# Two steps of a Strassen-like gate-and-up product change places: P3 of the first column group goes ahead of P2 of the second, and the first group's results are turned behind P3 of the second

## The chip, the cores and the metric

One core of a Trainium2 chip runs the whole kernel as one program. The metric is the device time of one execution in microseconds (us); the median of three runs of the kernel before is 1392.69 us (1392.04 to 1393.3).

## The reference, cut to what matters

The model is a two-layer encoder trunk on a sequence of 512 frames of width 1024, all in float32. Layer 0 has a mixer of gated linear attention and RWKV-7, layer 1 has multi-head latent attention; after each mixer stand a layer norm, a dense SwiGLU feed-forward block and another layer norm. The change touches only the first half of the two feed-forward blocks:

```python
gu = x @ w_gate_up                       # (512, 1024) @ (1024, 5632)
gate, up = gu[..., :2816], gu[..., 2816:]
y = (jax.nn.silu(gate) * up) @ w_down    # (512, 2816) @ (2816, 1024)
x = layer_norm(DN_ALPHA * x + y, ln_g, ln_b)
```

## The kernel before, in words

Every float32 product is made of three matmuls on rounded parts: an operand is cast to a high part on ScalarE (`wh`, L191) and the rest is subtracted on VectorE (`wl`, L192), both in `split`; TensorE then takes high times high, high times low and low times high.

`ffn` (L1139) computes gate and up for six groups of columns (`GROUPS`: four of 512, two of 384). For each group it uses a scheme of the Strassen kind with seven products, P1 to P7, in place of eight. `A` (L1161) holds the seven left operands made from quarters of x; those of P3, P5 and P6 lie in `Sh`/`Sl`, the others in `xh`/`xl`. `sink` (L1184) makes them from the transposed rows of x as the layer norm before yields them, on ScalarE and VectorE.

The right operands are weights in three raw tiles for each group: X, Y and Z. `step(name)` (L1273) does one product. Each product has two halves (`k2` = 0 and 1 in `product`, L1224): a half splits 1024 columns of the raw tile and feeds 12 matmuls, the first eight with the high part, the last four with the low part. Once P1, P3, P7 and P6 have split their operand, `more` (L1261) sends a GpSimd DMA for each half that adds further weights from memory into the same raw tile. Y is so used four times in a row: P3 splits it, a DMA adds to it, P7 splits it, a DMA adds, P6 splits it, a DMA adds, P4 splits it. P2 is added to P1's PSUM banks and P4 to P7's.

The split parts have two places each (`wh`, `wl`, `bufs=2`). With `spare` true, every third half (by `count`) goes to a third place called `third`, cut out of two tiles of `hid` (`parts`, L1211).

What a product yields is combined in the second half of `step`: P1 and P3 are copied out on ScalarE, P2 gets its Silu there, and P5, P6 and P4 are combined on VectorE (`dve`, L1270): P6 alone needs eight operations, which end in `w` (finished) and `v`; P4 finishes `v`. `turn(0)` (L1308) then transposes `w` of two row blocks on TensorE into PSUM tiles of tag "s", of which there are two, and ScalarE copies them into `hid` (L1315); `turn(1)` does so with `v`.

`load` fetches X, Z and Y of groups 0 and 1 on SP's queue long before they are used; `begin` does P1 of group 0 inside the stage before; `work` (L1330) does the rest. For groups 2 to 5 the order is P1, P4 of the group before, turn(0), P3, turn(1), P2, loads, P7, P5, P6. Groups 0 and 1 differ, since their P1 and P2 come first of all: then P3, P7, P5, P6 of group 0, and P4 of group 0, turn(0), P3 of group 1, turn(1), loads, P7 of group 1, and so on.

The source gives the order of importance. The framework lists the instructions of each engine by it and by its own estimate of when each is ready, so neighbouring steps can be woven into each other. On the chip each engine then runs its list in that fixed order.

Of the kernel before, what the change touches and what calls it, by code (L numbers as in the profile page):

```python
# [1138 lines left out]
def ffn(g, i, hid, ep):  # L1139
# [179 lines left out]
    gs = [group(j) for j in range(len(GROUPS))]  # L1319
# [10 lines left out]
    def work():  # L1330

        gs[1].step("P1", False)
        gs[0].step("P2", False)
        gs[1].step("P2", False)
        last = len(gs) - 1
        for j, x in enumerate(gs):
            more = j < 4
            if j:
                if j > 1:
                    x.step("P1", more)  # L1340
                gs[j - 1].step("P4", more)
                gs[j - 1].turn(0)
            x.step("P3", more)
            if j:
                gs[j - 1].turn(1)
            if j > 1:
                x.step("P2", more)
            if 0 < j < last:
                gs[j + 1].load("Z")
                gs[j + 1].load("X")  # L1350
                gs[j + 1].load("Y")
            x.step("P7", more)
            x.step("P5", more)
            x.step("P6", more)
        gs[last].step("P4", False)
        return [lambda h=h: gs[last].turn(h) for h in range(2)]

    return Ctx.of(sink=sink, again=again, load=load, begin=begin, work=work)


# [454 lines left out]
```

## Time and profile before

| what | value |
|---|---|
| median of three runs | 1392.69 us |
| profiled execution: its own time | 1392.04 us |
| profiled execution: span | 1390.0 us |
| mean granted TensorE clock | 0.99 |
| PE busy | 1339.4 us (96%) |
| DVE busy | 920.7 us (66%) |
| ACT busy | 686.5 us (49%) |
| POOL busy | 233.4 us (17%) |
| gate-and-up of layer 0 | from about 403 us of the span |
| gate-and-up of layer 1 | from about 1025 to 1260 us |

PE, DVE, ACT and POOL are TensorE, VectorE, ScalarE and GpSimd. A busy share of 96% means little by itself, since matmuls overlap; 512 columns start every 0.23 us at full clock. What counts is where PE waits, for whom, and at which granted clock it runs.

### The profile page before, as it was taken

What the parts mean: (1) busy time and instruction counts of PE and PEld (TensorE: products, weight loads), DVE (VectorE), ACT (ScalarE), POOL (GpSimd) and SP (SyncE); (2) the same over time, 40 slices, a digit from 0 to 9 for tenths busy, and PEclk for the clock granted to TensorE, in tenths of its full rate; (3) what the DMA queues carried; (4) which work ended last, traced back from release to release, by engine and by line L of the source; (5) the groups of instructions that cost most, each with busy time, mean ns of one, the idle gap of its engine ahead of it and who ended that gap; (6) DMA issues with size and microseconds to landing.
All of it is one profiled execution on the core that took longest, in us unless ns stands there. A gap on an engine that the chain in (4) does not pass through costs nothing.

```text
span 1390.0 us, 21743 instructions
## 1 busy us (share of the span) xinstructions
PE 1339.4 (96%) x8382; PEld 1060.7 (76%) x8382; DVE 920.7 (66%) x1704; ACT 686.5 (49%) x1212; POOL 233.4 (17%) x278
## 2 busy tenths in 40 slices
PE   8899999999999999999999999999999899999997
PEld 6577777766677788997888877666677788997886
DVE  3687677644496766667556367988785766667456
ACT  6653344455536455555344346555445455555341
POOL 2230021132311111127301220000001111120000
PEclk9999999989999999999999999999999999999999
DMA  7563343531478787763225321111367787773232
GB/s 243 114 125 60 74 100 72 105 65 46 145 221 198 157 189 166 151 125 97 91 93 157 109 94 47 53 55 46 117 163 190 155 193 167 145 127 93 91 107 90
DMA packets 74328, 168.15 MB, mean 121 GB/s; under 512 B 21232, under 2 KB 22384, under 8 KB 74096
## 3 DMA queue, kind: packets, MB, share of 16 engines
q0 software_dynamic: 21888, 60.83, 26.2%
q1 hardware_dynamic: 51808, 103.83, 22.6%
q10 hardware_dynamic: 528, 2.10, 0.4%
q8 instruction: 66, 1.08, 0.3%
q14 instruction: 38, 0.31, 0.1%
HBM read 163.77 MB, written 2.95 MB: 120 GB/s over the span
## 4 chain that ended last, share of the span: by engine, by line
PE 55%; DVE 4%; DMA 4%; issue 4%; ACT 2%; POOL 1%; SPq 0%; DVEq 0%; ACTq 0%; POOLq 0%
PE ps_g L1236 23%; PE ps_g L186 8%; PE ps_g L185 8%; PE ps_g L187 8%; PE ps_s L1617 3%; DMA raw<-in_w_gu 2%; PE ps_o L1646 2%; PE ps_t L1633 1%; PE ps_s L1314 1%; DMA wl<-in_w_mi 1%; DVE wl L192 1%; ACT wh L191 1%; DVE w L1270 0%; DMA w<-in_w_mo 0%; DVE x L1008 0%
## 5 line engine op out<-in xcount | busy, mean ns | idle before, releaser
L192 DVE TENSOR_TENSOR wl<-raw,wh 128x1024 fp32r<-128x1024 f32 (+1 forms) x116 | 127.6, 1111 | 87.7 <-ACT wh L191 87.7
L191 ACT CAST wh<-raw 128x1024 fp32r<-128x1024 f32 (+1 forms) x116 | 111.6, 967 | 140.7 <-PE ps_g L1236 94.9
L1263 POOL DMA_DIRECT2D raw<-in_w_gu x96 | 83.3, 869 | 496.9 <-DVE wl L192 274.0
L1236 PE MATMUL ps_g<-wh,xh 128*128 128x512 f32 (+1 forms) x312 | 115.9, 372 | 2.1 <-ACT wh L191 2.1
L187 PE MATMUL ps_g<-xh,wl 128*128 128x512 f32 (+2 forms) x296 | 113.2, 382 | 3.3 <-DMA wl<-in_w_even 2.2
L1236 PE MATMUL ps_g<-wh,xl 128*128 128x512 f32 (+1 forms) x312 | 114.8, 368 | 0.0
L185 PE MATMUL ps_g<-xh,wh 128*128 128x512 f32 (+2 forms) x296 | 114.6, 387 | 0.0
L186 PE MATMUL ps_g<-xl,wh 128*128 128x512 f32 (+2 forms) x296 | 113.3, 383 | 0.0
L186 PE MATMUL ps_g<-wl,ah 128*128 128x512 f32 x288 | 112.0, 390 | 0.6 <-DVE wl L192 0.6
L185 PE MATMUL ps_g<-wh,ah 128*128 128x512 f32 x288 | 111.7, 392 | 0.5 <-ACT ah L191 0.4
L187 PE MATMUL ps_g<-wh,al 128*128 128x512 f32 x288 | 110.8, 389 | 0.0
L192 DVE TENSOR_TENSOR wl<-w,wh 128x1024 fp32r<-128x1024 f32 (+2 forms) x79 | 89.4, 1132 | 31.9 <-ACT wh L191 31.4
L191 ACT CAST wh<-w 128x1024 fp32r<-128x1024 f32 (+2 forms) x79 | 76.3, 966 | 61.4 <-PE ps_g L186 36.5
L191 ACT CAST ah<-hid 128x512 fp32r<-128x512 f32 x72 | 43.7, 621 | 98.8 <-PE ps_g L186 98.8
L192 DVE TENSOR_TENSOR al<-hid,ah 128x512 fp32r<-128x512 f32 x72 | 49.4, 697 | 60.7 <-ACT ah L191 60.7
L1236 PE MATMUL ps_g<-wh,Sh 128*128 128x512 f32 (+1 forms) x232 | 87.1, 376 | 0.0
L1236 PE MATMUL ps_g<-wh,Sl 128*128 128x512 f32 (+1 forms) x232 | 86.7, 374 | 0.0
L1236 PE MATMUL ps_g<-wl,xh 128*128 128x512 f32 (+1 forms) x312 | 78.2, 372 | 4.1 <-DVE wl L192 4.1
L215 POOL DMA_DIRECT2D wl<-in_w_even x48 | 41.6, 867 | 227.0 <-ACT wl L214 191.9
L216 ACT CAST wh<-w 128x512 fp32r<-128x512 f32 x64 | 39.4, 618 | 81.2 <-PE ps_g L186 49.4
L187 PEld LDWEIGHTS ps_g<-xh,wl 128*128 128x128 f32 (+1 forms) x296 | 55.8, 189 | 14.9 <-DMA wl<-in_w_even 3.4
L1236 PEld LDWEIGHTS ps_g<-wh,xh 128*128 128x128 f32 x312 | 58.6, 188 | 10.6 <-ACT wh L191 3.2
(462 smaller groups left out, 3293.2 us busy)
## 6 DMA issues: line engine op xcount, KB each, us to landing
raw<-in_w_gu POOLq DMA_DIRECT2D x64, 512.0 KB, 5.6
w<-in_w_dn SPq DMA_DIRECT2D x44, 512.0 KB
raw<-in_w_gu SPq DMA_DIRECT2D x32, 512.0 KB
w<-in_w_even SPq DMA_DIRECT2D x48, 256.0 KB
wl<-in_w_even POOLq DMA_DIRECT2D x48, 256.0 KB, 4.7
raw<-in_w_gu POOLq DMA_DIRECT2D x32, 384.0 KB, 4.8
w<-in_w_gu SPq DMA_DIRECT2D x12, 512.0 KB
raw<-in_w_gu SPq DMA_DIRECT2D x16, 384.0 KB
```

The lines of the kernel that those rows point to most:

```text
L185: nc.tensor.matmul(out, lhsT=wh, rhs=xh, start=first, stop=False)
L186: nc.tensor.matmul(out, lhsT=wh, rhs=xl, start=False, stop=False)
L187: nc.tensor.matmul(out, lhsT=wl, rhs=xh, start=False, stop=last)
L191: c = nc.scalar.copy(h, src)
L192: (eng or nc.vector).tensor_tensor(l, in0=src, in1=h, op=ALU.subtract)
L215: nc.gpsimd.dma_start(l, src, accum_op=ALU.add)
L216: nc.scalar.copy(h, w)
L1236: nc.tensor.matmul(acc[u][:, :n], lhsT=A_[a][:, k, P * u:P * u + P], rhs=w[:, q], start=first and k + a + b == 0, stop=k + b == 4, skip_gr ...
L1263: nc.gpsimd.dma_start(T[k][k2], w[r, q, k2], accum_op=ALU.add)
L1314: nc.tensor.transpose(out=p[:, m * P:(m + 1) * P], in_=y[:, m * P:(m + 1) * P], identity=g.C("ident"))
L1617: nc.tensor.matmul(p[:, :nk], lhsT=Q[:, h % 4, qb * P:(qb + 1) * P], rhs=K[:, h % 4, :nk], start=True, stop=True)
L1646: nc.tensor.matmul(o[64 * e:64 * e + 64, kb * P:], lhsT=Vv[:, kb, (h - 1 + e) * 64:(h + e) * 64], rhs=t[e][kb][:, kb * P:], start=kb == 0, ...
```

## The change

`work` gets P3 of group 0 between the P2 of group 0 and that of group 1; it is no longer the first step of the loop, and its `spare` is now false, so that `third` is first used by a later half. In the round of group 1, `turn(0)` of group 0 no longer stands between P4 of group 0 and P3 of group 1, but behind that P3, directly ahead of `turn(1)`. Groups 2 to 5 keep their order. Both feed-forward blocks use this code.

```diff
         gs[1].step("P1", False)
         gs[0].step("P2", False)
+        gs[0].step("P3", False)
         gs[1].step("P2", False)
         last = len(gs) - 1
         for j, x in enumerate(gs):
             more = j < 4
             if j:
                 if j > 1:
                     x.step("P1", more)
                 gs[j - 1].step("P4", more)
-                gs[j - 1].turn(0)
-            x.step("P3", more)
-            if j:
-                gs[j - 1].turn(1)
+                if j > 1:
+                    gs[j - 1].turn(0)
+                x.step("P3", more)
+                for h in range(0 if j == 1 else 1, 2):
+                    gs[j - 1].turn(h)
             if j > 1:
                 x.step("P2", more)
```

## Rows read from the trace of the kernel before

**Rows 1.** Timeline of PE: start us, us, engine line op, out<-in xcount [idle before <-releaser].

```profile
456.44 1.07 PE L1236 MATMUL ps_g<-third,xh 128*128 128x512 f32 x4
...
458.83 0.63 PE L1314 MATMUL ps_s<-cst,w 128*128 128x128 f32 x4 [1.33 <-DVE w L1270]
460.64 0.63 PE L1314 MATMUL ps_s<-cst,w 128*128 128x128 f32 x4 [1.18 <-DVE w L1270]
461.02 0.51 PE L1236 MATMUL ps_g<-wh,Sh 128*128 128x512 f32 x1
...
468.15 1.03 PE L1314 MATMUL ps_s<-cst,v 128*128 128x128 f32 x8
468.94 0.48 PE L1236 MATMUL ps_g<-third,xh 128*128 128x512 f32 x1
...
1093.39 0.47 PE L1236 MATMUL ps_g<-third,xh 128*128 128x512 f32 x1
```

**Rows 2.** Windows: us, busy (x) of PE, PEld, DVE, ACT, POOL, PEclk, DMA, GB/s.

```profile
457.35:461.02 3.67, 1.17 (x9) 0.83 (x9) 3.67 (x7) 0.59 (x1) 0.00 (x0) 1.00 0.69 239
461.33:464.74 3.41, 3.41 (x10) 2.63 (x8) 3.41 (x6) 1.79 (x3) 1.35 (x2) 0.50 0.44 44
1085.97:1089.38 3.41, 3.41 (x10) 2.64 (x8) 3.41 (x6) 1.55 (x3) 1.59 (x2) 0.50 0.46 54
400.73:403.50 2.77, 2.19 (x17) 1.63 (x15) 2.70 (x5) 2.07 (x4) 0.00 (x0) 1.00 0.79 293
469.00:600.00 131.00, 131.00 (x641) 113.59 (x640) 88.07 (x107) 71.45 (x97) 25.16 (x29) 1.00 0.78 164
```

**Rows 3.** Chain that ended last, 400:545: start us, us, what.

```profile
430.02 1.24 DVE wl L192
...
431.54 5.34 DMA raw<-in_w_gu
...
448.10 5.17 DMA raw<-in_w_gu
```

**Rows 4.** Timeline of DVE.

```profile
426.57 1.22 DVE L192 TENSOR_TENSOR third<-raw,third 128x1024 fp32r<-128x1024 f32 x1
...
460.41 1.22 DVE L192 TENSOR_TENSOR wl<-raw,wh 128x1024 fp32r<-128x1024 f32 x1
...
1047.71 2.36 DVE L192 TENSOR_TENSOR wl<-hid,wh 128x1024 fp32r<-128x1024 f32 x2
...
1051.24 1.22 DVE L192 TENSOR_TENSOR wl<-raw,wh 128x1024 fp32r<-128x1024 f32 x1
...
1068.92 1.22 DVE L192 TENSOR_TENSOR wl<-raw,wh 128x1024 fp32r<-128x1024 f32 x1 [1.51 <-ACT wh L191]
...
1084.81 1.22 DVE L192 TENSOR_TENSOR wl<-raw,wh 128x1024 fp32r<-128x1024 f32 x1
```

**Rows 5.** Timeline of ACT.

```profile
467.40 1.05 ACT L191 CAST third<-raw 128x1024 fp32r<-128x1024 f32 x1 [3.91 <-DMA raw<-in_w_gu]
468.36 1.07 ACT L1291 COPY w<-ps_g 128x512 f32<-128x512 f32 x2
469.31 1.09 ACT L1315 COPY hid<-ps_s 128x512 f32<-128x512 f32 x2
...
1059.57 1.05 ACT L191 CAST third<-raw 128x1024 fp32r<-128x1024 f32 x1 [1.55 <-DMA raw<-in_w_gu]
...
1091.81 1.05 ACT L191 CAST third<-raw 128x1024 fp32r<-128x1024 f32 x1 [3.91 <-DMA raw<-in_w_gu]
```

**Rows 6.** Timeline of POOL.

```profile
1052.75 0.86 POOL L1263 DMA_DIRECT2D raw<-in_w_gu  x1 [0.27 <-DVE wl L192]
...
1072.40 0.86 POOL L1263 DMA_DIRECT2D raw<-in_w_gu  x1 [3.83 <-issue]
```

**Rows 7.** Timeline of PE, two earlier waits.

```profile
402.07 1.15 PE L1181 MATMUL ps_s<-cst,x 128*128 128x128 f32 x8 [0.29 <-ACT full L1172]
...
424.91 0.50 PE L1236 MATMUL ps_g<-third,Sh 128*128 128x512 f32 x1 [0.59 <-ACT third L191]
```

## The prediction, made before the changed kernel ran

> **What bounds the kernel now.** I read the waits of TensorE first, one stage after the other. In gate-and-up nearly all of them lie where groups 0 and 1 meet; from P7 of group 1 on, PE does not idle at all over 131 us of layer 0 [rows 2], and layer 1 looks the same. So whatever moves the start of that P7 moves the end of the kernel by as much, as long as nothing new waits behind it. It starts at 468.94 in layer 0 and at 1093.39 in layer 1 [rows 1].
>
> Ahead of it the timeline of PE shows the wait that the change goes for: turn(0) of group 0 stands still for 1.33 us, does four transposes, waits 1.18 us more for `w`, and only then P3 of group 1 may begin [rows 1]. Between P4's last matmul and P3's first lie 3.67 us with eight transposes in them, and right behind, the granted clock reads 0.50, the 1.2 GHz level, for 3.41 us, in both layers [rows 2]. A half-clock stretch of that length costs half of it, 1.7 us. That is 2.51 us idle and 1.7 us slow for each layer, 8.4 us in all, and a first look would book them.
>
> The chain of waits says otherwise, and it is the view to trust here. In layer 0 it does not run over PE from 430 to 460 us but over raw tile Y of group 0: P3's second half is subtracted at 430.02, its DMA lands 5.34 us after issue at 431.54, P7 casts and subtracts, a DMA again, P6, a DMA issued at 448.10 that takes 5.17, then P4 [rows 3]. Behind P4's last subtraction stand P6's eight VectorE operations, and behind these, at 460.41, the first subtraction of P3 of group 1 [rows 4]. Its DMA in turn frees the cast of P7 at 467.40, for which ScalarE waited 3.91 us [rows 5]. P7 of group 1 can't start before that cast ends at 468.45; it started at 468.94. So with the chain where it is, taking the wait ahead of P3 away would bring less than half a microsecond: PE would wait ahead of P7 instead.
>
> **The change, part by part.** *P3 of group 0 earlier.* The matmuls, casts and DMAs stay the same in number; they move. In layer 0 VectorE is the bound up to about 429 us, and does its subtractions there in a run of four; P3's first half has the third place in it, at 426.57, and the second half comes last, at 430.02 [rows 3, 4]. Now P3 takes the second and third place. Its second half then begins at about 426.57, 3.45 us earlier. Its low part goes to an ordinary place and not to `third`, which needs the low matmuls of P2's second half done; they are four. The two DMAs then follow each other within 1.1 us, and where they do so in layer 1, the second lands later: issued at 1052.75 [rows 6], cast at 1059.57 [rows 5], 6.82 us against 5.34, so 1.48 us are lost. Left: 1.97 us. The bounds are 0 (P3's second half gets no earlier place) and 3.45.
>
> In layer 1 the subtractions of P2 of group 1 at 1047.71 (two of them) stand ahead of those of P3, the last of which is at 1051.24 [rows 4]; exchanged, P3's last stands at 1048.85, 2.39 us earlier. Further down the chain, P6's second half is subtracted by 1070.14 (1068.92 and 1.22) [rows 4], and 0.29 us is what such a DMA needs after its subtraction (1051.24 and 1.22 against 1052.75). It was issued at 1072.40 behind a wait that the profile puts down to nothing [rows 6]: 1.97 us lost. I take it as an accident that does not come back, with 0 as the other bound. Together 4.36 us.
>
> The P2 of group 1 that now stands behind P3 is off the chain. Its Silu on ScalarE frees banks that P6 needs, two products later. PE itself has to wait about as long as before in that stretch, 0.59 us at 424.91 [rows 7]: P3's left operand is among the last things `sink` makes. I count nothing, with 1 us to either side in each layer.
>
> *turn(0) behind P3 of group 1.* PE goes from P4 straight into P3. Its eight high matmuls run at once, its low ones wait for the subtraction behind the eight operations, at 460.41 less 1.97 in layer 0. So part of the old wait comes back inside P3, but off the chain. Then turn(0) finds `w` finished long before.
>
> What is late next is the cast of P7: 467.40 less 1.97 is 465.43, its end 466.48, against a start at 468.94: 2.46 us gained. In layer 1 the cast at 1091.81 [rows 5] goes to 1087.45, its end to 1088.50, against 1093.39: 4.89 us. But turn(1) had been done by then and now hasn't. It needs the two PSUM tiles of turn(0), which ScalarE copies out only behind P7's cast and behind P3's copies of `w`, as rows 5 list them (467.40, 468.36, 469.31). So I place turn(1) among the first matmuls of P7, for its own 1.03 us [rows 1] and 0.29 us of waiting for a tile, as in the one place where four such transposes come in a row [rows 7]. Net: 1.14 us in layer 0, 3.57 us in layer 1, 4.71 us together. If the copies come out ahead of that cast, turn(1) fits into the wait and each layer gains 1.32 more.
>
> *The clock.* From P3's last matmul to P7's first there are now two turns and a wait. P3's end: the subtraction's end (459.66 in layer 0, 1081.67 in layer 1) and 16 matmuls at 0.23 us, so 463.3 and 1085.3; P7 comes 3.2 us later in both. Without matmuls but with transposes, 3.67 us brought the clock down, and 2.77 us (400.73 to 403.50) did not [rows 2]. 3.2 lies between, so I charge one of the two layers with 1.7 us, bounds 0 and 3.4.
>
> The Trainium skill, in "TensorE: Matmul & The Clock Gate", section "Why this matters for your kernels", warns that idle between bursts of matmuls brings the clock back down, which speaks against putting all four turns into one place. The rows agree that a gap does it; by that rule alone both layers pay, and the sum would be 1.3 us of gain.
>
> The skill's "DMA: Bandwidth & Descriptors", section on the anatomy of a DMA through GpSimd, gives 2.0 us plus bytes over 436 per ns, an estimate of 3.2 us for such a half of 512 KB. The trace disagrees, with 5.17 to 5.34 us for these, which add as they write; by the page the chain would not bind, and the sum would be the first rival's.
>
> *The sum.* 4.71 less 1.7 is 3.0 us. The profiled execution took 1392.04 us, so 1389.0; the median lies 0.65 us above it: 1389.7 us.
>
> **Rivals.** *All of it is gained.* The chain moves far enough that PE alone counts: 8.4 us less two waits of 0.29 us for a PSUM tile is 7.8, so 1384.9 us. For it: P3's second half could gain up to 3.45 us in layer 0. Against it: rows 3 leave no slack at any link.
>
> *Nothing comes of it.* The framework had already woven P3's first half into P2 of group 1 (its first matmul at 424.91 [rows 7]), so the first edit is partly there already. If the unexplained 1.97 us come back and both layers pay the clock, 4.71 less 1.97 less 3.4 is 0.7 us slower: 1393.4 us, within 0.2%.
>
> *Slower.* PE's list has turn(1) ahead of P7, while ScalarE's list has the copies of turn(0) behind P7's cast. Then P7 waits for the cast (1.05 us), the two copies of `w` (1.07), those of turn(0) (1.09) and four transposes (0.52): 3.73 us after the DMA lands, 469.2 in layer 0 (0.2 later than before) and 1091.2 in layer 1 (2.2 earlier). Both layers fall to half clock, 3.4 us: 1.4 us slower. With the 1.97 us in layer 1 back, 3.4 us: 1396.1 us. It decides as soon as the chain gains less than about 2.5 us for a layer. For it: rows 5 show that order on ScalarE. Against it: a list made by readiness puts P7's matmuls, free by then, ahead of a transpose that isn't.
>
> **How the numbers follow.** About 0.2% (2.8 us) is what a measurement of this kernel can tell from no change. Forecast 0.43, all gained 0.20, nothing 0.25, slower 0.12. The forecast's own cases run from 1.3 us of gain (both layers slow) to 7.4 (no slow stretch, both turns hidden); 0.29 of its 0.43 gain over 2.8 us. With the first rival that is 0.49 for faster; slower gets 0.11, of the last rival; the rest, 0.40, is within. The range reaches from 1384.3, just past the first rival, to 1393.8, just past the second; the last rival is left out.
>
> **What would show it.** Right: no wait of turn(0) for `w`; P7 of group 1 about 2.5 us (layer 0) and 4.9 us (layer 1) earlier, each right behind its cast; ScalarE still waiting there for a DMA; turn(1) inside P7; P3 split ahead of P2 of group 1. Wrong: P7 of group 1 with its raw tile landed well ahead, or a turn that waits for a ScalarE copy for a microsecond; the slow clock gone in both layers, or there in both; a new gap between P2 of group 1 and P7 of group 0.

## The result, and the profile after

The changed kernel is slower by 0.7%: 1400.73 us median of eight runs (1396.97 to 1406.88) against 1392.68 us of the kernel before in the same rounds, a ratio of 1.007 with a 95% interval of 1.0044 to 1.0097. The forecast was 1389.7 us, in a range up to 1393.8.

The profiled execution took 1405.09 us, with a span of 1403.0, 13.0 us more than before. Not all of that is the change. The clock in the first mixer, which is the same code, granted 0.50 for 20.5 us in this execution and for 10.2 us in that of before; this alone makes some 5 us (10.2 at half speed), and gate-and-up of layer 0 begins 4.6 us later. So I compare by stage: from the first matmul of line 1236 to the first transpose of turn(0) of group 1, by which time all work of group 0 is done. Before, that is 403.50 to 496.26 us in layer 0, 92.76 us. After, it is 97.04 us in layer 0, and in layer 1 it is 99.32 against 95.81 (1024.91 to 1120.72): 4.28 and 3.51 us longer, 7.8 us in all. Outside these two stages the executions differ by 0.6 us more, besides that later start. The windows of the two stages after (columns as in [rows 2]):

```profile
408.13:520.00 111.87, 102.82 (x466) 82.64 (x467) 77.35 (x95) 61.53 (x85) 19.03 (x22) 1.00 0.79 182
1034.11:1150.00 115.89, 105.23 (x477) 84.11 (x476) 79.95 (x102) 62.43 (x87) 17.30 (x20) 1.00 0.70 157
```

The granted clock stays at its upper level throughout: both half-clock stretches of [rows 2] are gone, and with them 3.4 us of slower work, so the waits of PE have grown by more than its time. That does not mean that the change would have gained 3.4 us: before, P7 of group 1 began only 0.49 and 0.53 us behind the end of its cast [rows 1, 5], so a quicker P3 would for the most part have waited there. The waits of PE in layer 0, 425:500, after (us in total, times, longest):

```profile
PE ps_g L1236 <- DVE wl L192: 3.3, 2, 2.2
PE ps_g L1236 <- ACT wh L191: 2.5, 2, 1.4
PE ps_g L1236 <- ACT third L191: 1.9, 1, 1.9
PE ps_s L1314 <- ACT hid L1315: 0.5, 1, 0.5
```

In the same window before there were 2.5 us for `w` and 0.6 for `third`; 3.1 us have become 8.2. The wait of turn(0) for `w` is gone, as the change wants; waits for the split of weights have come in its place. Where they stand on PE, after:

```profile
442.07 0.50 PE L1236 MATMUL ps_g<-wh,xh 128*128 128x512 f32 x1 [1.45 <-ACT wh L191]
...
459.77 0.50 PE L1236 MATMUL ps_g<-wh,xh 128*128 128x512 f32 x1 [1.05 <-ACT wh L191]
...
469.48 1.20 PE L1236 MATMUL ps_g<-wl,Sh 128*128 128x512 f32 x4 [2.15 <-DVE wl L192]
...
473.24 1.03 PE L1314 MATMUL ps_s<-cst,w 128*128 128x128 f32 x8
...
476.16 0.50 PE L1236 MATMUL ps_g<-third,xh 128*128 128x512 f32 x1 [1.88 <-ACT third L191]
...
477.62 1.15 PE L1314 MATMUL ps_s<-cst,v 128*128 128x128 f32 x8 [0.49 <-ACT hid L1315]
```

In order these are P7 of group 0, P4 of group 0, the low part of P3 of group 1, turn(0), P7 of group 1, and turn(1) inside that P7. The last four answer to [rows 1]; they came in the order that was forecast, but later in the stage. The first two were not forecast, and they are new. (The other wait for `wl` in the list, 1.15 us at 430.12, stands where 0.59 us stood before [rows 7], within what the prediction allowed there.) ScalarE's timeline after tells why the first two came:

```profile
440.02 1.05 ACT L191 CAST third<-raw 128x1024 fp32r<-128x1024 f32 x1 [3.48 <-DMA raw<-in_w_gu]
440.97 1.99 ACT L191 CAST wh<-raw 128x1024 fp32r<-128x1024 f32 x2
...
458.68 1.04 ACT L191 CAST wh<-raw 128x1024 fp32r<-128x1024 f32 x1 [5.15 <-DMA raw<-in_w_gu]
461.17 1.05 ACT L191 CAST third<-raw 128x1024 fp32r<-128x1024 f32 x1 [1.45 <-DMA raw<-in_w_gu]
...
475.06 1.04 ACT L191 CAST third<-raw 128x1024 fp32r<-128x1024 f32 x1 [3.77 <-DMA raw<-in_w_gu]
```

The cast at 440.02 is that of P7's second half, the first user of `third` now; the cast of P7's first half comes behind it, at 440.97. Layer 1 shows the same swap (1066.68 and 1067.63). The DMA of the second half is issued last and lands last, and the first half's cast waits for it, though its own DMA, issued at 431.74, landed 5.8 us later, 3.4 us ahead of that cast. Before, ScalarE cast the first half (the first of the two at 433.58) ahead of the second:

```profile
433.58 2.01 ACT L191 CAST wh<-raw 128x1024 fp32r<-128x1024 f32 x2 [1.81 <-DMA raw<-in_w_gu]
...
436.90 1.05 ACT L191 CAST third<-raw 128x1024 fp32r<-128x1024 f32 x1 [0.35 <-DMA raw<-in_w_gu]
```

The order on POOL after:

```profile
431.74 0.85 POOL L1263 DMA_DIRECT2D raw<-in_w_gu  x1 [14.09 <-ACT wh L191]
432.93 0.86 POOL L1263 DMA_DIRECT2D raw<-in_w_gu  x1 [0.34 <-DVE wl L192]
442.62 0.86 POOL L1263 DMA_DIRECT2D raw<-in_w_gu  x1 [8.83 <-DVE third L192]
443.75 0.86 POOL L1263 DMA_DIRECT2D raw<-in_w_gu  x1 [0.28 <-DVE wl L192]
453.17 0.86 POOL L1263 DMA_DIRECT2D raw<-in_w_gu  x1 [8.55 <-DVE third L192]
455.08 0.86 POOL L1263 DMA_DIRECT2D raw<-in_w_gu  x1 [1.05 <-DVE wl L192]
469.72 0.86 POOL L1263 DMA_DIRECT2D raw<-in_w_gu  x1 [13.78 <-DVE wl L192]
```

P3's two DMAs go out early, at 24.80 us of the stage for the second, against 28.04 before. But P7's are issued 1.13 us apart and in the wrong order, the second half first. Before, they stood 3.31 us apart, the first half first:

```profile
436.19 0.86 POOL L1263 DMA_DIRECT2D raw<-in_w_gu  x1 [3.79 <-DVE wl L192]
439.50 0.86 POOL L1263 DMA_DIRECT2D raw<-in_w_gu  x1 [2.46 <-DVE third L192]
```

P6's first half now waits for the later of the two: its cast stands at 450.56, 6.81 us behind the DMA issued at 443.75.

### The profile page after: what moved, and what is told of

Same layout as the page of the kernel before. It is cut to its first block, busy times and chain, and to the rows that moved or that the text cites. A ratio compares the mean times of both kernels' runs of the same rounds, so it can differ in the third digit from the quotient of the medians.

```text
span 1403.0 us, 21752 instructions
## 1 busy us (share of the span) xinstructions
PE 1343.7 (96%) x8382; PEld 1061.9 (76%) x8382; DVE 921.0 (66%) x1704; ACT 684.8 (49%) x1212; POOL 229.7 (16%) x278
```

## The experiments

The table gives the time of the stage, measured as above in one profile each, the half-clock stretches that lie in it (3.41 us each, 1.7 us of slower work), and the ratio of device times to the kernel before, timed beside it. No kernel was profiled twice, so how far a stage varies by itself is not known; half-clock stretches come and go between the rows, and differences of a microsecond or less should not be read. The intervals of the times are some 3 to 6 us to each side.

| kernel | layer 0, us | layer 1, us | sum less before | half-clock stretches | ratio (95%) |
|---|---|---|---|---|---|
| before | 92.76 | 95.81 | 0 | 1 and 1 | |
| changed | 97.04 | 99.32 | +7.8 | 0 and 0 | 1.007 (1.0044 to 1.0097) |
| e1 | 96.13 | 97.67 | +5.2 | 1 and 2 | 1.0032 (1.0007 to 1.0057) |
| e2 | 93.08 | 96.12 | +0.6 | 1 and 1 | 1.0023 (0.9995 to 1.0051) |
| e3 | 93.02 | 94.70 | -0.9 | 1 and 0 | 0.9994 (0.9966 to 1.0022) |
| e4 | 94.86 | 97.11 | +3.4 | 1 and 1 | 1.0017 (0.9988 to 1.0046) |
| e5 | 88.63 | 91.10 | -8.8 | 0 and 1 | 0.9938 (0.9915 to 0.9962) |
| e6 | 87.70 | 89.48 | -11.4 | 0 and 0 | 0.9936 (0.9896 to 0.9976) |
| e7 | 93.12 | 94.55 | -0.9 | 0 and 1 | 0.9988 (0.996 to 1.0015) |
| e8 | 94.71 | 95.96 | +2.1 | 0 and 1 | 1.0034 (1.0007 to 1.0062) |

**e1, the first edit alone** (against the kernel before):

```diff
         gs[0].step("P2", False)
+        gs[0].step("P3", False)
         gs[1].step("P2", False)
...
-            x.step("P3", more)
             if j:
+                x.step("P3", more)
                 gs[j - 1].turn(1)
```

> Only the first edit: P3 of group 0 ahead of P2 of group 1; turn(0) stays ahead of P3 of group 1. Theory A (order of the casts: with `third` idle, ScalarE's list has the cast of P7's second half, whose DMA lands last, ahead of that of its first half): P7 of group 0 starts about 2.4 us late, P4 waits 1 to 2 us for its cast, and the kernel is 5 to 8 us slower than before. Theory B (the move of turn(0) is what costs): no slower than before, 0 to 3 us faster.

5.2 us slower by stage, 1.0032 in time (some 4 us). In layer 0 ScalarE has the same swapped casts, and P7 of group 0 waits for its cast as after the change, with turn(0) where it was before (waits of PE, 420:490):

```profile
440.89 1.05 ACT L191 CAST third<-raw 128x1024 fp32r<-128x1024 f32 x1 [3.79 <-DMA raw<-in_w_gu]
441.84 1.99 ACT L191 CAST wh<-raw 128x1024 fp32r<-128x1024 f32 x2
```

```profile
PE ps_g L1236 <- ACT wh L191: 2.4, 2, 1.8
PE ps_s L1314 <- DVE w L1270: 2.4, 2, 1.2
PE ps_g L1236 <- DVE wl L192: 1.1, 1, 1.1
```

So theory A holds for the first edit, which makes 5.2 of the 7.8 us by itself.

**e2, the second edit alone** (against the kernel before):

```diff
                 gs[j - 1].step("P4", more)
-                gs[j - 1].turn(0)
+                if j > 1:
+                    gs[j - 1].turn(0)
             x.step("P3", more)
             if j:
-                gs[j - 1].turn(1)
+                for h in range(0 if j == 1 else 1, 2):
+                    gs[j - 1].turn(h)
```

> Only the second edit: turn(0) of group 0 behind P3 of group 1, P3 of group 0 where it was. Theory A: within 2 us of before; P7 of group 1 waits for its cast, whose DMA lands at the same time as before, and P7 of group 0 starts as before. Theory B: 6 to 8 us slower, as the full change.

0.3 us slower in each layer by stage, and in time no change is within the interval; both half-clock stretches are back. The waits in layer 0, 420:490:

```profile
PE ps_g L1236 <- DVE wl L192: 2.1, 1, 2.1
PE ps_g L1236 <- ACT third L191: 0.8, 2, 0.6
PE ps_s L1314 <- ACT hid L1315: 0.5, 1, 0.5
```

The 2.51 us of turn(0) have become 2.1 us inside P3 of group 1 and 0.5 us of turn(1). The second edit moves a wait and removes none. Theory B falls. By stage e1 and e2 make 5.9 us together; the other 2.0 come only when both edits meet, and were not taken apart.

**e3, the full change with `third` for P2 of group 1:**

```diff
         gs[0].step("P3", False)
-        gs[1].step("P2", False)
+        gs[1].step("P2")
```

> The full change, but P2 of group 1 may use `third` for its first half, so that P7's second half has to wait for that place and its cast is listed behind that of the first half. Theory A: P7 of group 0 loses its 1.2 to 1.5 us wait for the cast, the DMAs of its halves go out apart again, and the kernel is 2 us slower to 4 us faster than before, so 6 to 12 us faster than the full change. Theory B: no more than 2 us faster than the full change.

The whole loss is gone: 8.6 us less than the full change by stage. The ninth half, the first of P2 of group 1, now takes `third`; the twelfth, P7's second, has to wait until TensorE is done with it. ScalarE casts in the right order, and the DMAs of P7 (432.60 and 435.15) stand apart again:

```profile
430.00 1.05 ACT L191 CAST wh<-raw 128x1024 fp32r<-128x1024 f32 x1 [2.45 <-DMA raw<-in_w_gu]
430.95 1.07 ACT L1291 COPY w<-ps_g 128x512 f32<-128x512 f32 x2
432.55 1.05 ACT L191 CAST third<-raw 128x1024 fp32r<-128x1024 f32 x1 [0.53 <-PE ps_g L1236]
```

```profile
432.60 0.86 POOL L1263 DMA_DIRECT2D raw<-in_w_gu  x1 [4.96 <-DMA raw<-in_w_gu]
435.15 0.86 POOL L1263 DMA_DIRECT2D raw<-in_w_gu  x1 [1.70 <-DVE third L192]
```

P7's first half is cast 28.89 us into the stage, against 32.84 after the change and 30.08 before.

**e4, the full change with P7 of group 0 in ordinary places:**

```diff
-            x.step("P7", more)
+            x.step("P7", more and j > 0)
```

> The full change, but P7 of group 0 uses the ordinary places for both halves, so that its casts are listed in order with `third` still idle until then. Theory A: the 1.2 to 1.5 us wait ahead of P7 of group 0 gets shorter by at least 1 us, and the kernel is 3 to 10 us faster than the full change. Theory B: within 2 us of the full change.

4.4 us less than the full change by stage, though with two half-clock stretches that the changed kernel doesn't have. `third` idles until a later product, the order of the casts is put right, and P7's wait is gone. The cast of its first half comes 29.68 us into the stage:

```profile
430.15 1.05 ACT L191 CAST wh<-raw 128x1024 fp32r<-128x1024 f32 x1 [1.25 <-DMA raw<-in_w_gu]
432.64 1.05 ACT L191 CAST wh<-raw 128x1024 fp32r<-128x1024 f32 x1 [1.43 <-DMA raw<-in_w_gu]
```

So the swapped order costs, and it isn't all: e4 stays 3.4 us above before, where e3 does not.

**e8, the kernel before with P3 of group 0 in ordinary places:**

```diff
-            x.step("P3", more)
+            x.step("P3", more and j > 0)
```

> The kernel before, with P3 of group 0 in the ordinary places; nothing moved. Theory A: `third` is idle until P7 here too, but P3 stands between, so the casts of P7 are listed in order: within 1.5 us of before. Rival (the lost third place is what costs): 3 to 8 us slower than before.

Not within 1.5 us: 2.1 us by stage, 1.0034 in time. In layer 0 both halves of P3 now wait for an ordinary place and are cast together. The first half's DMA goes out 28.06 us into the stage, against 24.58 before, and the second's 1.14 us behind it instead of 3.46, so that P7 waits 1.7 us for its cast (waits of PE, 420:490):

```profile
PE ps_s L1314 <- DVE w L1270: 2.4, 2, 1.2
PE ps_g L1236 <- ACT wh L191: 1.7, 1, 1.7
PE ps_g L1236 <- ACT third L191: 0.7, 1, 0.7
```

So the lost third place costs by itself, as the rival has it, though by stage less than the rival's 3 to 8 us, and less than e1 with its swapped casts (5.2). The times, 1.0034 and 1.0032, do not tell the two apart. In layer 1 it costs next to nothing (0.15 us).

**e7, the first edit alone with `third` for P2 of group 1:** e1 with the edit of e3.

> Only the first edit, as e1, with `third` for P2 of group 1. Theory A: turn(0) of group 1 comes 2 to 4 us earlier in each layer than in e1, and no later than before; the kernel is 0 to 4 us faster than before. Rival (P3 early itself is late, by the missing third place for P3 or by `sink`): within 2 us of e1, so 3 to 6 us slower than before.

0.9 us faster by stage, 0.9988 in time, whose interval includes no change; 6.1 us better than e1 by stage. In layer 0 turn(0) of group 1 comes 0.36 us later than before, where theory A had it no later. Beside e3 (-0.9) it shows what the second edit brings once the casts are in order: nothing that can be seen. The waits for `w` of 1.04 and 1.18 us in e7 are 0.68 us for P3's low part, 1.69 us for P7's cast and 0.5 us for a tile of turn(1) in e3.

**e6, P3 of group 1 ahead of P4 of group 0**, P3 of group 0 where it was before:

```diff
-            acc[name] = p = acc[chained] if chained else banks(name == "P5" or name == "P1" and j != 1)
+            acc[name] = p = acc[chained] if chained else banks(name == "P5" or name == "P1" and j != 1 or name == "P3" and j == 1)
...
-            if j:
-                if j > 1:
-                    x.step("P1", more)
+            if j == 1:
+                x.step("P3", more)
+                gs[0].step("P4", more)
+                gs[0].turn(0)
+            elif j:
+                x.step("P1", more)
                 gs[j - 1].step("P4", more)
                 gs[j - 1].turn(0)
-            x.step("P3", more)
-            if j:
+            if j != 1:
+                x.step("P3", more)
+            if j > 1:
                 gs[j - 1].turn(1)
...
             x.step("P7", more)
+            if j == 1:
+                gs[0].turn(1)
```

> P3 of group 0 where it was before, P3 of group 1 ahead of P4 of group 0 as in e5. If the chain binds: 4 to 9 us faster than before, within 2 us of e5. If P3 of group 0 has to go early for that: at least 3 us slower than e5.

The first line puts P3 of group 1 into the two PSUM banks of P5. By the count, `third` also goes to P3's second half where P4's had it.

1376.13 us against 1387.54 of the kernel before beside it, 0.9936 in time (some 9 us); 11.4 us less by stage, which is more than the 4 to 9 us expected. All waits at the meeting of the groups are gone; of PE's waits in layer 0, 420:490, one line is left, the old one ahead of P3 of group 0 [rows 7]:

```profile
PE ps_g L1236 <- ACT third L191: 0.6, 1, 0.6
```

P3 of group 1 needs nothing from tile Y of group 0, so it is split, and its matmuls begin (446.19), while the second of P6's DMAs for P4 (issued at 442.24) is still under way. Its own DMAs go out well before P7 of group 1 needs them, and P6's eight VectorE operations have P3 and P4 to hide behind. ScalarE's cast for P7 of group 1, in e6, stands ahead of turn(0)'s copies and is done 4.4 us before PE needs it (P7 begins at 457.86):

```profile
452.36 1.06 ACT L191 CAST third<-raw 128x1024 fp32r<-128x1024 f32 x1 [3.11 <-DMA raw<-in_w_gu]
...
457.71 0.59 ACT L1315 COPY hid<-ps_s 128x512 f32<-128x512 f32 x1 [0.29 <-PE ps_s L1314]
```

Layer 1 gains more (6.33 us against 5.06): there PE had also waited 1.45 us for the cast of P4 of group 0 before, and in e6 it does not.

**e5, e3's first part and e6's second:** `gs[0].step("P3", False)` ahead of `gs[1].step("P2")`, with the rest as in e6.

> P3 of group 0 early with `third` for P2 of group 1, as in e3, and P3 of group 1 ahead of P4 of group 0, into the two banks of P5; turn(0) of group 0 behind that P4, turn(1) behind P7 of group 1. If the chain over tile Y and P6's eight VectorE operations is what still binds there (theory A's second half), PE loses its waits ahead of P3 and P7 of group 1 and turn(0) of group 1 comes 3 to 5 us earlier in each layer: 5 to 9 us faster than before. If the waits there come from TensorE's own work or from the banks, no more than 2 us faster.

0.9938 in time, level with e6 (0.9936); 8.8 us less by stage, 2.6 us behind e6, with one half-clock stretch more. P3 of group 0 early adds nothing.

## Why the prediction was wrong

The reading of the kernel before held. The chain over tile Y binds, not PE: e2 shows that without its wait for `w`, PE waits elsewhere, and e6, which takes group 1's P3 out of that chain, gains more by stage (11.4 us) than the 8.4 us of idle and slow time that the prediction counted.

*P3's second half earlier: right.* Forecast 3.45 us in layer 0 and 2.39 in layer 1, measured 3.24 (24.80 against 28.04) and 2.16 (25.68 against 27.84). *Its DMA slower when two go together: right.* 7.09 us from 432.93 to the cast at 440.02, against 5.34; the cast of P7's second half came 1.51 us earlier, forecast 1.97.

*Every later link moves with it: this step failed.* The prediction let P7, P6 and P4 follow P3's second half as before, 1.97 us earlier in layer 0 and 4.36 in layer 1. It did not follow the count that gives out `third`. Every third half may take it: before, that was the ninth, P3's first half, and the twelfth, P7's second. Moved up, P3's halves are the seventh and eighth, and the ninth is the first of P2 of group 1, whose `spare` is false. So `third` lies idle until the twelfth, while P7's first half needs an ordinary place. This comes from the move: with `spare` true P3's two halves would have got ordinary places all the same, so the change's new `False` on P3 does nothing, although the section on the change gives it as the reason. The framework lists by its own estimate of readiness, and lists the cast of P7's second half first. On the chip the first half's cast then waits for a later DMA: it comes 2.76 us later than before (32.84 against 30.08), where the prediction had the links of this chain come earlier. From there P7's DMAs go out as a pair, and in layer 1 the next cast waits for the second of it:

```profile
1077.42 1.05 ACT L191 CAST third<-raw 128x1024 fp32r<-128x1024 f32 x1 [5.49 <-DMA raw<-in_w_gu]
```

Its DMA was issued at 1070.41, 7.01 us before. The cast of P7 of group 1 ends up 3.03 us later in layer 0 and 2.33 in layer 1, not 1.97 and 4.36 earlier. The sign that the prediction named came, a new gap between P2 of group 1 and P7 of group 0: 1.45 us at 442.07. e4, which changes P7's place and with it the order of the casts, takes more than half of the loss away; e3, which also gives `third` a user again, takes all of it.

The Trainium skill, "TensorE: Matmul & The Clock Gate", section "Architectural detail: the array is 16× 32×32, not 1× 128×128", says that ScalarE and VectorE work off their queues strictly in order. The trace agrees: the cast at 440.97 stands behind one that waited 3.48 us.

*The lost third place was costed at nothing: wrong.* The prediction said that P3's low part goes to an ordinary place, and asked only whether that place is free. e8 takes the place from P3 with the steps in their old order: 2.1 us by stage. What it costs in the new order, apart from the swap, was not measured.

*The second edit: right.* P3's low part waits in turn (2.15 us), turn(0) waits for nothing, P7 starts right behind its cast (476.16 against 475.06 and 1.04), and turn(1) falls into it with a wait of 0.49 us for a tile, 0.29 forecast. The rival in which turn(1) goes ahead of P7 did not come.

*The clock: wrong, the other way.* One stretch of 1.7 us was charged; none came in either layer, and the two of before went.

*POOL's 1.97 us in layer 1 as an accident: wrong.* They stand in all ten traces, at the same DMA, that of P6's second half in layer 1; after the change again 1.96 us (1081.64 and 0.29 to 1083.89):

```profile
1080.41 1.23 DVE L192 TENSOR_TENSOR wl<-raw,wh 128x1024 fp32r<-128x1024 f32 x1 [0.69 <-ACT wh L191]
```

```profile
1083.89 0.86 POOL L1263 DMA_DIRECT2D raw<-in_w_gu  x1 [3.01 <-issue]
```

The last rival had the right sign but another mechanism; none of the four held what happened.

What stays open: why the framework lists the second half first. That it does is read from ScalarE's timelines, and e3, e4 and e7 show what it costs; its estimates were not seen. The stage of e4 is 3.4 us above before; the 2.1 us of e8 may be part of that, but this was not taken apart, nor were the 2.0 us by which the two edits together lose more than each alone.

## What to carry to other kernels

Where a scheduler lists instructions by its own estimate of readiness, an extra buffer that falls idle is not neutral: here a later piece was listed ahead of an earlier one, and on ScalarE, which worked its list in order, the earlier one then waited for the later one's data. When steps are moved, follow the rotation of every buffer (here a count of halves) through to the new order, and look at the compiled order of each engine at the moved place. And when a chain of transfers binds, moving a wait along it gained nothing (e2); a product that needs nothing of the chain, put into its gaps, took away the waits that the chain had caused (e6).

## What the hardware showed that was not expected

Two 512 KB additions from memory issued within 1.2 us of each other went with a late second one, and this the prediction had charged: 7.09 and 7.01 us from issue to its cast after the change, 6.82 in layer 1 before, against 5.3 to 6.4 us for the six of group 0 in layer 0 before, which stand over 3 us apart.

Half-clock stretches (granted 0.50, which is 1.2 GHz) do not follow the waits closely. After the change, turn(0), a wait of 1.88 us, three matmuls, and turn(1) with a wait of 0.49 us left the clock at its upper level. In e3 the same work in the same order, with waits of 1.69 and 0.50 us, saw it fall at turn(1) and stay down for 3.41 us (TensorE's timeline of e3; the eight transposes took 1.15 us after the change):

```profile
463.54 0.50 PE L1236 MATMUL ps_g<-third,xh 128*128 128x512 f32 x1 [1.69 <-ACT third L191]
...
465.00 1.97 PE L1314 MATMUL ps_s<-cst,v 128*128 128x128 f32 x8 [0.50 <-ACT hid L1315]
```

POOL's wait of 1.97 us at one DMA of layer 1 is in every kernel, and the profile names no cause.
